# A hyena, conformer and attention encoder: its 64x64 transform done in pairs on quarters of TensorE

## The chip, the cores and the metric

The kernel runs on one core of a Trainium2 chip. The time is the device time of one execution in microseconds (us); every output is float32. One execution of each kernel is also profiled, and the rows below come from that.

## The reference, cut to what matters

One encoder layer runs over two request groups (x_prompt, x_sample) of 2048 positions and 1024 channels, with the same weights:

```
h = rmsnorm(x);  p = h @ w_in                         # 1024 -> 3584
hyena:     u, z = conv3(p_u) split in x0, x1, v
           k2 = two-sided filter from an MLP, on a circle of 4096, (4096, 512)
           y = x0 * (irfft(rfft(v*x1, 4096) * rfft(k2)) + skip*(v*x1))   # 512 channels
conformer: GLU, conv over 31 positions, layernorm, silu                 # 256 channels
attention: 4 heads of 64 into 256 memory tokens                         # 256 channels
out = rmsnorm(x + concat(y*silu(z) of the three) @ w_out)
```

The long convolution is the part that the change touches: a Fourier transform of 4096 points for each of 512 channels and two groups, a product with the filter's spectrum, and the inverse.

## The kernel before, in words

The 4096 points are a 64 x 64 matrix of n1 and n2. The two groups are taken as real and imaginary part of one complex sequence, so one transform serves both. It has four steps: stage A transforms over n1 for each n2 (result X1, in DRAM, by n2 and k1); stage B takes one k1 at a time, transforms over n2, multiplies with the filter's spectrum and transforms back over k2 (result AA, in DRAM, by k1 and n2); stage C transforms back over k1 for each n2 and goes on to the output.

The program has four stretches.

Stage 1 (0 to about 1370 us) is the projection h @ w_in in 5184 matmuls of 128x512 (lines 502 to 504), split in high and low parts. Beside it, queues of background steps (`fq` and others) give TensorE and the rest their small work: the conformer's convolution on VectorE (L276), the filter's MLP and its transform over n1 (`spec`, L400, into XF in DRAM, 16 calls), and the first 8 stage A's (`trans` in `a_background`). u = v*x1 goes to UU in DRAM at L558, for 4 tiles of channels and two groups.

Attention (about 1370 to 1516) has 16 blocks (`attention`, L841), of 512 positions each. Beside them come the other 24 stage A's (`stage_a`, L897), two for each of the first 12 blocks. A stage A transposes, multiplies in three split products (`times_t1`), moves its two PSUM results to SBUF, one on ScalarE and one on VectorE (L912), and stores them.

Stage B (about 1494 to 1682) has 33 steps t. Steps 1 to 31 handle k1 = t and k1 = 64-t, which share one spectrum, steps 0 and 32 one k1. `spectrum` makes K from XF with a full 128x128 matmul (L932) and copies it in four halves (L934 to L937). `unit` is then called for each k1: a full 128x128 matmul (L918), two copies that swap the halves of its result (L920, L921), u*kr on VectorE (L923), us*ki on VectorE or POOL (L924), their sum or difference on POOL (L925), the inverse matmul (L927), a copy (L928) and one store of 128 partitions x 2 KB. All these are float32 matmuls, which the trace shows as two instructions each. Every third step from t = 9 also loads and splits a slice of w_out (`wo_load`, L943; the splits are L234 on ScalarE and L235 on POOL). The last two blocks of attention are mixed with the first four steps of stage B.

Stage C (1682 to about 2104) has 32 steps n of two n2 each: it loads its slices of AA (`at`), of GG (the gate, `g8`), of x, transforms (L1034), transposes (L1039), gates (L1043), splits, and projects with w_out in 48 matmuls (L1057 to L1059), adds x and normalizes.

What sets the order: a scheduler at build time puts each engine's instructions in one list by estimated times; within `in_order()` the order in which the code is written holds for PE and ScalarE. Each engine executes its list in that order. Loads are issued on SP's queue, stores of stage B on ScalarE's. Eight semaphores serve the transfers of both queues in turn, and a transfer waits for the one that had its semaphore before to land. Tiles come from rings: a tile of a tag with bufs=n waits for the n-th one before it to be released.

## Time and profile before

| | us |
|---|---|
| median of three runs | 2107.04 |
| lowest and highest | 2104.28, 2109.05 |
| profiled execution | 2107.82 |
| its span in the trace | 2106.0 |
| PE busy | 1983.5 (94%) |
| DVE busy | 1233.5 (59%) |
| ACT busy | 780.4 (37%) |
| POOL busy | 847.8 (40%) |

PE is TensorE's matmuls, DVE VectorE, ACT ScalarE, POOL GpSimd, SP the engine that issues the loads. The times of PE count pipelined matmuls and are not a measure of its peak. The share of the span is an average over stretches with different limits, so the rows below are asked of single stretches.

### The profile page before, as it was taken

The page shows a single profiled execution, that of the slowest core. Times are in us where ns is not written, and L with a number is a line of the kernel's source. Part 1 is how long each engine was busy: PE and PEld are TensorE (multiplying, and loading weights), DVE is VectorE, ACT ScalarE, POOL GpSimd, SP SyncE. Part 2 cuts the span into 40 slices and gives each one's busy share as a digit, 9 for nine tenths or more (in the row PEclk, how much of TensorE's full clock was granted, in tenths as well). Part 3 has the DMA queues.
Part 4 walks back from the last instruction along what each step waited for, and adds up shares of the span by engine and source line. Part 5 has one row for each costly group of instructions (what it writes and reads, how often), then busy time and mean ns, then how long its engine had stood idle before and what let it go on. Part 6 is the DMA issues. An engine that isn't in the chain of part 4 may idle for free. (4 is left out here: it accounts for less than half of the span.)

```text
span 2106.0 us, 25970 instructions
## 1 busy us (share of the span) xinstructions
PE 1983.5 (94%) x8866; PEld 1500.1 (71%) x8866; DVE 1233.5 (59%) x1779; ACT 780.4 (37%) x1468; POOL 847.8 (40%) x838
## 2 busy tenths in 40 slices
PE   5999989998998999999998999899988899999998
PEld 5887778777887787777776877777533267777776
DVE  4533974959646379445448865278887624344443
ACT  4422112131335244444431222278688622222221
POOL 3332766554543222344434441266598711111110
PEclk8999999999999999999999999999999999999999
DMA  9634134342458323233341325698888685555552
GB/s 333 210 106 158 68 93 116 99 133 80 171 191 278 131 86 108 82 96 84 102 116 56 118 88 189 221 291 263 245 273 273 215 218 135 152 159 148 152 145 61
DMA packets 238558, 328.72 MB, mean 156 GB/s; under 512 B 87177, under 2 KB 117913, under 8 KB 236634
## 3 DMA queue, kind: packets, MB, share of 16 engines
q1 hardware_dynamic: 146026, 260.72, 38.9%
q10 hardware_dynamic: 87056, 54.57, 9.6%
q0 software_dynamic: 5344, 11.77, 2.0%
q8 instruction: 71, 1.16, 0.2%
q14 instruction: 61, 0.50, 0.1%
HBM read 196.37 MB, written 130.61 MB: 155 GB/s over the span
## 5 line engine op out<-in xcount | busy, mean ns | idle before, releaser
L502 PE MATMUL pj<-xh,whi 128*128 128x512 f32 (+1 forms) x1728 | 679.0, 393 | 23.6 <-ACT xh L468 6.7
L503 PE MATMUL pj<-xl,whi 128*128 128x512 f32 (+1 forms) x1728 | 673.4, 390 | 9.7 <-POOL xl L469 9.7
L504 PE MATMUL pj<-xh,wlo 128*128 128x512 f32 (+1 forms) x1728 | 671.8, 389 | 2.0 <-POOL wlo L235 2.0
L276 DVE SCALAR_TENSOR_TENSOR bg<-bg,vb,bg 128x512 f32<-128x512 f32 x480 | 399.0, 877 | 39.6 <-POOL bg L271 35.7
L502 PEld LDWEIGHTS pj<-xh,whi 128*128 128x128 f32 x1728 | 332.3, 193 | 105.2 <-ACT sm L516 15.0
L503 PEld LDWEIGHTS pj<-xl,whi 128*128 128x128 f32 x1728 | 332.8, 193 | 79.7 <-POOL xl L469 11.0
L504 PEld LDWEIGHTS pj<-xh,wlo 128*128 128x128 f32 x1728 | 332.5, 192 | 71.0 <-issue 3.6
L1057 PE MATMUL ms<-wo,mh 128*128 128x512 f32 x512 | 204.3, 399 | 2.2 <-ACT mh L234 2.2
L1058 PE MATMUL ms<-wo,mh 128*128 128x512 f32 x512 | 201.2, 393 | 0.0
L1059 PE MATMUL ms<-wo,ml 128*128 128x512 f32 x512 | 194.3, 397 | 0.2 <-POOL ml L235 0.2
L516 ACT COPY sm<-pj 128x512 f32<-128x512 f32 x96 | 56.5, 589 | 353.4 <-PE pj L504 272.0
L525 DVE SCALAR_TENSOR_TENSOR sm<-sm,va,sm 128x448 f32<-128x448 f32 (+1 forms) x96 | 77.7, 809 | 145.5 <-POOL sm L523 106.0
L544 POOL TENSOR_TENSOR big<-big,sm 128x448 f32<-128x448 f32 (+1 forms) x64 | 121.2, 1894 | 100.9 <-DVE sm L527 100.9
L1060 DVE TENSOR_TENSOR xr<-xr,ms 128x512 f32<-128x512 f32 x64 | 44.0, 688 | 199.0 <-PE ms L1059 198.9
L523 POOL TENSOR_SCALAR sm<-sm,va 128x448 f32<-128x448 f32 (+1 forms) x96 | 110.9, 1155 | 114.3 <-ACT sm L516 110.6
L241 POOL TENSOR_TENSOR ss<-ss,mhalf 128x1 f32<-128x1 f32 x32 | 17.7, 553 | 313.3 <-DVE ss L240 313.3
L1057 PEld LDWEIGHTS ms<-wo,mh 128*128 128x128 f32 x512 | 96.9, 189 | 47.4 <-issue 24.3
L1059 PEld LDWEIGHTS ms<-wo,ml 128*128 128x128 f32 x512 | 96.5, 188 | 21.0 <-DVE mf L1043 0.8
L1058 PEld LDWEIGHTS ms<-wo,mh 128*128 128x128 f32 x512 | 96.9, 189 | 20.0
L239 ACT ACTIVATE junk<-xr 128x1024 bf16<-128x1024 f32 x32 | 33.9, 1060 | 192.4 <-DVE xr L1060 185.9
L925 POOL TENSOR_TENSOR z<-z,us 128x512 f32<-128x512 f32 x64 | 81.9, 1289 | 31.3 <-DVE us L924 22.7
L235 POOL TENSOR_TENSOR wlo<-sm,whi 128x512 fp32r<-128x512 f32 x50 | 75.6, 1526 | 37.2 <-ACT whi L234 28.9
(169 smaller groups left out, 2758.6 us busy)
## 6 DMA issues: line engine op xcount, KB each, us to landing
big<-in_xt_dram SPq DMA_DIRECT2D x32, 512.0 KB, 6.8
in<-x1d SPq DMA_DIRECT2D x128, 128.0 KB, 3.6
aa<-o ACTq DMA_DIRECT2D x64, 256.0 KB, 3.5
at<-aa SPq DMA_DIRECT2D x64, 256.0 KB, 5.0
out_dram<-xr ACTq DMA_DIRECT2D x64, 256.0 KB, 3.8
sm<-in_win_dram SPq DMA_DIRECT2D x52, 256.0 KB, 3.6
ws<-whi SPq DMA_DIRECT2D x52, 256.0 KB, 3.0
ws<-wlo SPq DMA_DIRECT2D x52, 256.0 KB, 4.2
```

The source lines that it names most:

```text
L235: (sub_eng or nc.gpsimd).tensor_tensor(lo, src, hi.bitcast(F32), op=ALU.subtract)
L276: nc.vector.scalar_tensor_tensor(st["a", c], st["h", c][:, k:k + TB], vb[:, 2 * k + c:2 * k + c + 1], st["a", c], op0=ALU.mult, op1=ALU.add)
L502: nc.tensor.matmul(ps[:, ts_], hi, xh[:, k, ts_], start=k == 0, stop=False)
L503: nc.tensor.matmul(ps[:, ts_], hi, xl[:, k, ts_], start=False, stop=False)
L504: nc.tensor.matmul(ps[:, ts_], lo, xh[:, k, ts_], start=False, stop=k == KC - 1)
L523: nc.gpsimd.tensor_scalar(ct[:, o:e], pt[:, o + 1:e + 1], w[1], va[:, 52 + ch:53 + ch], op0=ALU.mult, op1=ALU.add)
L525: nc.vector.scalar_tensor_tensor(ct[:, o:e], pt[:, o:e], w[0], ct[:, o:e], op0=ALU.mult, op1=ALU.add)
L544: nc.gpsimd.tensor_tensor(v, v, out, op=ALU.mult)
L925: nc.gpsimd.tensor_tensor(z, z, us, op=op)
L1057: nc.tensor.matmul(po, mh[:, k, :], woh[k][:, hs], start=i == 0, stop=False)
L1058: nc.tensor.matmul(po, mh[:, k, :], wol[k][:, hs], start=False, stop=False)
L1059: nc.tensor.matmul(po, ml[:, k, :], woh[k][:, hs], start=False, stop=i == 7)
```

## The change

The n2 are taken in the order (0, 32), (1, 33), ... Stage A's two results of a pair are replaced by their sum and difference (`butterfly`): ScalarE copies one result, VectorE adds the other to it and then subtracts. `spec` does the same. So the transform over n2 is left with 32 pairs, once for the even and once for the odd k2, and what was one 128x128 matrix falls apart into 64x64 quarters.

Stage B has 32 steps, each with a pair of k1, t and `mirror(t)` (64-t, and 32 for 0). `forward` transforms both with four quarter matmuls into two banks; `multiply` makes four products on VectorE, straight from PSUM; `inverse` forms the complex sums in the accumulation of eight quarter matmuls, in one tile of two banks, which ScalarE copies in one instruction and POOL adds and subtracts; `store` writes each k1 with 64 partitions x 4 KB. `spectra` makes K for two steps at once. AA has 1024 columns and 64 rows for each k1. PSUM pools change (tr 3 to 4, one two-bank `pa`, no `po`: attention's result o sits in `tr`), rings too (`in` 8 to 9, `z` and `k` 8, `o` 4 of 1024). Stage B starts after the block loop. UU is written in two transfers for one; in stage C g8 has four loads of 256-byte runs for two of 512-byte runs, and indices follow the new n2 order.

```diff
+    def butterfly(a, b, px):
+        nc.scalar.copy(b, px[1])
+        nc.vector.tensor_tensor(a, px[0], b, op=ALU.add)
+        nc.vector.tensor_tensor(b, px[0], b, op=ALU.subtract)
...
     def spec(b, n):
+                butterfly(f[0], f[1], px)
                 for q in range(2):
-                    nc.scalar.copy(f[q], px[q])
                     nc.sync.dma_start(XF[n2p // 2, q * P:(q + 1) * P, :], f[q])
...
-        ms, tr, pa, po_ = psum(c2, ms=2, tr=3, pa=2, po=1)
+        ms, tr = psum(c2, ms=2, tr=4)
+        pap = c2.enter_context(tc.tile_pool(reuse_waits="tile", name="psa", bufs=1, space=PS))
...
     def stage_a(n):
-            px = pa(), pa()
+            px = pa().rearrange("p (s c) -> p s c", s=2)
+            px = px[:, 0, :], px[:, 1, :]
             times_t1(px, th, tl, uh, ul)
+            xo = t_z(), t_z()
+            butterfly(*xo, px)
             for s in range(2):
-                xo = tl_("us", 4)
-                (nc.scalar.copy if s else nc.vector.tensor_copy)(xo, px[s])
-                nc.scalar.dma_start(X1[2 * n + s, 0:128, :], xo)
+                nc.scalar.dma_start(X1[2 * n + s, 0:128, :], xo[s])
...
+        def quarters(banks, jobs):
+            n = len(jobs[0][3])
+            for j in range(n):
+                for b, c, r, ops in jobs:
+                    w, x = ops[j]
+                    nc.tensor.matmul(banks[b][c, :], w[r, :], x[r, :], start=j == 0, stop=j == n - 1)
+        def spectra(ts):
...
+            for j in range(2):
...
+                    pk = [tr() for _ in ts]
+                    quarters(pk, [(i, c, (lo_, hi_)[(i + h) % 2], [(stab[:, 2 + 2 * i + j, :], xfs[i])])
+                                  for i in range(len(ts)) for h, c in enumerate((lo_, hi_))])
+                for b, p in enumerate(pk):
+                    k = t_k()
+                    nc.scalar.copy(k, p)
...
+        def forward(st, t):
+            xa, xb = fetch(t), fetch(mirror(t))
+            st["u"] = u = ms(), ms()
+            w0, w1 = stab[:, 0, :], stab[:, 1, :]
+            quarters(u, [(0, lo_, lo_, [(w0, xa)]), (0, hi_, hi_, [(w0, xa)]),
+                         (1, lo_, hi_, [(w1, xb)]), (1, hi_, lo_, [(w1, xb)])])
+        def multiply(st):
+            for j in range(2):
+                for b in range(2):
+                    st["z", j, b] = t_z()
+                    nc.vector.tensor_tensor(st["z", j, b], st["u"][b], st["k", j, b], op=ALU.mult)
+        def inverse(st, t):
+            o = pa()
+            quarters((o[:, 0:TB], o[:, TB:]),
+                     [(h, c, r, [(stab[:, 6 + 2 * v + j, :], st["z", j, v]) for j in range(2)])
+                      for h, c, r, v in ((0, lo_, lo_, 0), (0, hi_, hi_, 1), (1, lo_, hi_, 0), (1, hi_, lo_, 1))])
+            eo, st["y"] = tl_("o", 4, 1024), tl_("o", 4, 1024)
+            nc.scalar.copy(eo, o)
+            for h, op in enumerate((ALU.add, ALU.subtract)):
+                nc.gpsimd.tensor_tensor(st["y"][:, h * TB:(h + 1) * TB], eo[:, 0:TB], eo[:, TB:], op=op)
+        def store(st, t):
+            for k, r in ((t, lo_), (mirror(t), hi_)):
+                nc.scalar.dma_start(AA[k, 0:64, :], st["y"][r, :])
+        def stage_b():
+            sts = [{} for _ in range(33)]
+            spectra([(sts[0], 0)])
+            forward(sts[0], 0)
+            for t in range(33):
+                with in_order():
+                    if t < 32:
+                        if t:
+                            forward(sts[t], t)
+                        multiply(sts[t])
+                    if t % 2 == 0 and t < 31:
+                        spectra([(sts[k], k) for k in (t + 1, t + 2) if k < 32])
+                    if t:
+                        inverse(sts[t - 1], t - 1)
+                    if t > 1:
+                        store(sts[t - 2], t - 2)
+                    if t >= 9 and t % 3 == 0 and t < 32:
+                        wo_load(t // 3 - 3)
+            store(sts[31], 31)
...
             attention(*blocks[n], qy)
             more_a(1)
-            if n >= 14:
-                more_b(2)
             qy = nq
-        more_b(33)
+        stage_b()
...
-                g8 = sp.tile([P, 4, 2, P], F32, tag="g8", name=nm("g8"))
+                g8 = sp.tile([P, 4, 2, 2, 64], F32, tag="g8", name=nm("g8"))
                 for g in range(2):
-                    nc.sync.dma_start(g8[:, :, g, :], chans(GG, g, n))
+                    for q in range(2):
+                        nc.sync.dma_start(g8[:, :, g, q, :], chans(GG, g, q, n))
```

On PE, the end of stage B of the kernel before has each step's three kinds of matmul (tr is the forward, ms the spectrum, pa the inverse), here in steps 30 to 32:

```order
L918 MATMUL tr_13395<-in_13392,stab 128x512
L927 MATMUL pa_13359<-z_13355,stab 128x512
L932 MATMUL ms_13419<-in_13416,stab 128x512
L927 MATMUL pa_13387<-z_13383,stab 128x512
L918 MATMUL tr_13431<-in_13428,stab 128x512
L918 MATMUL tr_13448<-in_13445,stab 128x512
L932 MATMUL ms_13464<-in_13461,stab 128x512
```

The changed kernel has on PE, in two steps near the start of stage B (ms is the forward, tr the spectra, pa the inverse; x2 is two quarters):

```order
L964 MATMUL ms_12110<-in_12104,stab 64x512 x2
L964 MATMUL ms_12111<-in_12107,stab 64x512 x2
L964 MATMUL tr_12130<-in_12124,stab 64x512 x2
L964 MATMUL tr_12131<-in_12127,stab 64x512 x2
L964 MATMUL tr_12140<-in_12124,stab 64x512 x2
L964 MATMUL tr_12141<-in_12127,stab 64x512 x2
L964 MATMUL pa_12150<-z_12082,stab 64x512
L964 MATMUL pa_12150<-z_12084,stab 64x512
```

Every step now issues its forward first, then the spectra for the next two steps (in every second step), then the inverse of the step before, whose second half uses two more z; in the kernel before the three kinds came in an order that varied.

On DVE, one block of attention with its two stage A's in the kernel before (L859 is attention's maximum, L865 and L872 its normalization, L879 its gate; L235 and L912 are stage A's):

```order
L235 TENSOR_TENSOR k_1488_10787<-tr_10781,k_1487_10786 128x512
L865 RECIPROCAL se_10854<-se_10854 128x2
L865 RECIPROCAL se_10872<-se_10872 128x2
L912 COPY us_10767<-pa_10759 128x512
L872 COPY ynp<-tr_10838 128x4x128
L859 TENSOR_REDUCE mx_10956<-ms_10951 128x2
L859 TENSOR_REDUCE mx_10974<-ms_10969 128x2
L912 COPY us_10798<-pa_10790 128x512
```

The same place on DVE in the changed kernel, where L257 and L258 are the butterfly's sum and difference, L894 the maximum, L900 and L907 the normalization, L914 the gate:

```order
L907 COPY ynp<-tr_10578 128x4x128
L257 TENSOR_TENSOR z_10394<-pa_10387,z_10395 128x512
L894 TENSOR_REDUCE mx_10739<-ms_10734 128x2
L258 TENSOR_TENSOR z_10395<-pa_10387,z_10395 128x512
L900 RECIPROCAL se_10718<-se_10718 128x2
L914 TENSOR_TENSOR ynp<-tr_10404,z_10402 128x512
L907 COPY ynp<-tr_10618 128x4x128
L894 TENSOR_REDUCE mx_10757<-ms_10752 128x2
L900 RECIPROCAL se_10740<-se_10740 128x2
L257 TENSOR_TENSOR z_10506<-pa_10499,z_10507 128x512
L894 TENSOR_REDUCE mx_10842<-ms_10837 128x2
L900 RECIPROCAL se_10758<-se_10758 128x2
```

One L912 copy of each stage A has become two instructions, with attention's maximum between them, and both of them read the same two-bank tile pa.

On ACT, in stage B of the kernel before (L920 and L921 swap halves, L928 moves the inverse, L936 a half of K):

```order
L936 ACTIVATE k_2107_12895<-ms_12892 64x512
L920 COPY us_12906<-tr_12904 64x512
L921 COPY us_12906<-tr_12904 64x512
L928 COPY o_12855<-pa_12868 128x512
L920 COPY us_12923<-tr_12921 64x512
L921 COPY us_12923<-tr_12921 64x512
L980 DMA aa<-o_12855 128x512
```

On ACT, in two steps of the changed stage B (k are the spectra of two steps, o<-pa is eo):

```order
L1025 COPY o_12195<-pa_12186 128x1024
L1031 DMA aa<-o_12160 64x1024 x2
L989 COPY k_12234<-tr_12228 128x512
L989 COPY k_12236<-tr_12229 128x512
L989 COPY k_12244<-tr_12238 128x512
L989 COPY k_12246<-tr_12239 128x512
L1025 COPY o_12257<-pa_12248 128x1024
L1031 DMA aa<-o_12196 64x1024 x2
```

The two stores of a step stand behind the copy of the next step's inverse, and the seven half and full copies of a step before have become three on the mean.

## Rows read from the trace of the kernel before

**Rows 1.** Busy by stretch: length, PE, PEld, DVE, ACT, POOL, clock, DMA, GB/s
```profile
1378.00:1478.00 100.00, 100.00 (x756) 71.85 (x753) 82.42 (x166) 80.02 (x263) 61.52 (x77) 1.00 0.84 269
...
1516.00:1682.00 166.00, 140.74 (x296) 52.43 (x294) 126.49 (x176) 126.92 (x223) 138.46 (x107) 0.98 0.80 256
1682.00:1698.00 16.00, 9.77 (x35) 6.44 (x36) 1.09 (x3) 2.42 (x4) 1.30 (x1) 0.81 0.84 216
1698.00:2088.00 390.00, 389.51 (x1722) 293.71 (x1723) 155.45 (x215) 86.82 (x153) 56.92 (x61) 0.99 0.56 147
```

**Rows 2.** Groups by line in stage B: busy us, mean ns, idle before
```profile
L925 POOL TENSOR_TENSOR z<-z,us 128x512 f32<-128x512 f32 x61 | 78.1, 1290 | 25.1 <-DVE us L924 16.5 <-PE tr L918 2.6 <-PE pa L927 1.9
...
L923 DVE TENSOR_TENSOR z<-tr,k 128x512 f32<-128x512 f32 x60 | 41.0, 689 | 20.1 <-ACT us L921 12.7 <-POOL z L925 2.8 <-PE pa L927 2.6
L928 ACT COPY o<-pa 128x512 f32<-128x512 f32 x60 | 34.9, 587 | 12.5 <-PE pa L927 10.6 <-ACT o L928 0.8
...
L235 POOL TENSOR_TENSOR wo<-in,wo 128x512 fp32r<-128x512 f32 x16 | 21.5, 1352 | 2.4 <-ACT wo L234 2.3
```

**Rows 3.** Waits of stage B, 1516 to 1682: us in total, times, longest
```profile
PEld pa L927 <- POOL z L925: 21.9, 24, 3.2
...
POOL z L925 <- DVE us L924: 16.5, 10, 6.4
```

**Rows 4.** Waits of SP's queue, 1515 to 1682
```profile
SPq L954 <- DMA aa<-o: 30.5, 23, 4.9
```

**Rows 5.** DMA of stage B: total, issues, KB each, us to landing
```profile
DMA packets 24101, 42.43 MB, mean 256 GB/s; under 512 B 3831, under 2 KB 3831, under 8 KB 23957
...
aa<-o ACTq DMA_DIRECT2D x60, 256.0 KB, 3.5
in<-x1d SPq DMA_DIRECT2D x106, 128.0 KB, 3.5
```

**Rows 6.** Timeline of DVE: starts of L879, the end of an attention block
```profile
1468.91 0.69 DVE L879 TENSOR_TENSOR ynp<-po,o 128x512 f32<-128x512 f32 x1
...
1477.86 0.69 DVE L879 TENSOR_TENSOR ynp<-po,o 128x512 f32<-128x512 f32 x1
...
1485.22 0.69 DVE L879 TENSOR_TENSOR ynp<-po,o 128x512 f32<-128x512 f32 x1
...
1492.32 0.69 DVE L879 TENSOR_TENSOR ynp<-po,o 128x512 f32<-128x512 f32 x1 [0.33 <-PE po L877]
```

**Rows 7.** Timeline of PE in stage 1, about a spec
```profile
778.08 1.09 PE L405 MATMUL ms<-f,f 64*64 64x512 f32 x8
779.10 0.70 PE L356 MATMUL ms<-f,wf 128*128 128x256 f32 x2
```

**Rows 8.** Line 937 from 1540 to 1682: ns min/median/max, first and last start
```profile
L937 DVE COPY k<-ms x24: 694/695/696, 1542.5 to 1676.0; 64x512 f32<-64x512 f32 x24
```

**Rows 9.** Busy time by stretch, first 52 us
```profile
0.00:52.00 52.00, 27.82 (x153) 26.26 (x154) 22.86 (x53) 25.08 (x54) 15.94 (x20) 0.87 0.94 332
```

**Rows 10.** Page, group of L239
```profile
L239 ACT ACTIVATE junk<-xr 128x1024 bf16<-128x1024 f32 x32 | 33.9, 1060 | 192.4 <-DVE xr L1060 185.9
```

**Rows 11.** Page, DMA issues: KB each, us to landing
```profile
out_dram<-xr ACTq DMA_DIRECT2D x64, 256.0 KB, 3.8
```

**Rows 12.** Line 980: ns of one issue, min/median/max
```profile
L980 ACTq DMA_DIRECT2D aa<-o x33: 326/327/361, 1503.2 to 1682.7; - x33
```

**Rows 13.** Chain of waits at the end of stage B
```profile
1680.07 1.98 PE pa L927 x2
1682.07 0.59 ACT o L928
1682.69 5.59 DMA aa<-o
```

**Rows 14.** Busy time by stretch, second half of stage 1
```profile
700.00:1370.00 670.00, 651.62 (x2885) 513.85 (x2884) 383.30 (x529) 235.97 (x327) 233.93 (x283) 0.99 0.36 112
```

More of the change, by code (lines that the diff above doesn't have):

```diff
@@ new lines, in inverse, with both @@
+    def inverse(k2, conj, turned):
+        th = 2 * np.pi * ((k2[:, None] * ab.T) % 64) / 64
+        w = np.zeros((2, 32, 2, 32))
+        re = np.stack([np.cos(th), np.sin(th)], axis=1)
+        im = conj * np.stack([-np.sin(th), np.cos(th)], axis=1)
+        w[0], w[1] = (im, -re) if turned else (re, im)
+        return w.reshape(64, 64)
+    def both(a, b):
+        return np.concatenate([a, b], axis=0)
+    ev, od, evr, odr = 2 * jj, 2 * jj + 1, 62 - 2 * jj, 63 - 2 * jj
+    fk = both(forward(ev), forward(od))
@@ new lines, in _tables @@
+    kr, ki = np.tile(fk[:, :32], 2), np.tile(fk[:, 32:], 2)
+    turn = np.roll(np.arange(128), 64)
+    stab = np.stack([both(forward(ev), forward(od)), both(forward(evr, -1.0), forward(odr, -1.0)),
+                     kr, ki, kr[turn], ki[turn]] + [
+        both(inverse(ev, 1.0, u), inverse(od, 1.0, u)) for u in (False, True)] + [
+        both(inverse(odr, -1.0, u), inverse(evr, -1.0, u)) for u in (False, True)], axis=1)
+    sk = np.zeros((2, 32, 2, 4, 2, 2, 32))
+    for h in range(2):
+        k2 = 2 * jj + h
+        th, al = 2 * np.pi * ab * k2 / 64, np.pi * ab / 64 + 2 * np.pi * ab * k2 / 64
+        sg = (-1.0) ** h
+        g0, g1 = (np.cos(al), -np.sin(al)), (-sg * np.sin(al), -sg * np.cos(al))
+        for c_ in range(2):
+            for v in range(2):
+                sk[h, :, 0, 2 * c_, h, v] = (np.cos(th), -np.sin(th))[c_]
+                sk[0, :, 1, 2 * c_ + 1, h, v] = (g0[c_] + g1[c_]) / 2
+                sk[1, :, 1, 2 * c_ + 1, h, v] = (g0[c_] - g1[c_]) / 2
@@ new lines @@
+        lo_, hi_ = slice(0, 64), slice(64, 128)
+        def quarters(banks, jobs):
[5 more added lines that the diff above has]
+        def spectra(ts):
+            xfs = []
+            for i, (_, t) in enumerate(ts):
+                xfs.append(t_in())
+                src = XF[:, 0:256, :].rearrange("m (h e k) c -> m h e k c", h=2, e=4)
+                for h in range(2):
+                    r = 64 * ((h + i) % 2)
+                    nc.sync.dma_start(xfs[i][r:r + 64, :], src[:, h, :, t, :])
+            if ts[0][1] == 0:
+                sk = t_in().rearrange("p (j c) -> p j c", j=4)
+                nc.sync.dma_start(sk, a["sk"])
+            for j in range(2):
+                if ts[0][1] == 0:
+                    pk = tr(), tr()
+                    for b in range(2):
+                        nc.tensor.matmul(pk[b], sk[:, 2 * j + b, :], xfs[0], start=True, stop=True)
+                else:
+                    pk = [tr() for _ in ts]
[4 more added lines that the diff above has]
+                    nc.scalar.copy(k, p)
+                    if ts[0][1] == 0:
+                        ts[0][0]["k", j, b] = k
+                    else:
+                        ts[b][0]["k", j, 0] = ts[b][0]["k", j, 1] = k
```

136 lines of the change are left out of this document (45 added, 91 removed).

## The prediction

> **What bounds the kernel now.** I read the busy time by stretch first [rows 1]. Attention (1378 to 1478 us) keeps TensorE busy 100.00 of 100 us at full clock; stage C (1698 to 2088) 389.51 of 390. Between them lies stage B, 1516 to 1682, in which no engine is full: PE 140.74 of 166, DVE 126.49, ACT 126.92, POOL 138.46. The chain of waits runs through the end of stage B, the landing of its last store and into stage C [rows 13], so whatever shortens stage B shortens the kernel one for one, and whatever attention loses is lost one for one.
>
> What holds stage B is read next from its groups and waits. Its costliest group is POOL's add, 61 x 1290 ns [rows 2], and PE's largest wait is for just that: 21.9 us before the inverse matmul, while POOL itself waited 16.5 us for DVE's product [rows 3]. The loading queue on SP waited 30.5 us, in 23 places, for an earlier store to land [rows 4]. So three things share it: a long chain through four engines, POOL, and the DMA traffic at 256 GB/s [rows 5]. The rate of the stage is read from the one DVE copy that comes once a step: 24 of them from 1542.5 to 1676.0, so 133.5 / 23 = 5.80 us a step [rows 8].
>
> **The change part by part.** The new step T handles the same two k1 in 32 steps; I price each engine.
>
> PE: forward is four f32 64x64 quarters, inverse eight, the spectra eight in every second step (the order of PE shows the rows). Stage 1 has such quarters already: eight instructions, which are four f32 matmuls of two passes, take from 778.08 to 779.10, 1.02 us [rows 7]. So a group of four costs 1.02; a step has 1 + 2 + 1 (mean) groups, 4.1 us; a step with spectra 5.1, one without 3.1.
>
> DVE: four products of PSUM and K at 689 ns (L923 [rows 2]), 2.8 us. The copies to K and the DVE half of us*ki go. But both `ms` banks are held until the last two products have read them, and the next forward rewrites them: forward 1.1 + 4 x 0.69 = 3.9 us is a floor of each step. So pairs of steps take 5.1 + 3.9, mean 4.5.
>
> ACT: two copies of spectra at 587 ns (as L928 [rows 2]) and one of 128x1024, for which the nearest row is the 1060 ns of L239 [rows 10]: 2.2 us, and under 3 with the casts of w_out. POOL: two ops at 1290 ns and 16 splits of w_out at 1352 [rows 2] over 32 steps: 2.6 + 0.7 = 3.3 us.
>
> DMA: per step four X1 loads of 128 KB, two of XF, two stores of 256 KB and half a w_out load of 256 KB: 1408 KB, 1.44 MB. At the 256 GB/s of now that takes 5.6 us; at the 332 GB/s that the first 52 us reach, at a share of 0.94 [rows 9], 4.35. The share of now is 0.80 [rows 1]; stage B's own traffic at 0.94 would be 256 x 0.94 / 0.80 = 301 GB/s, 4.8 us. A store is now 64 partitions of 4 KB where it was 128 of 2 KB; out_dram<-xr has the new form and lands in 3.8 us against 3.5 [rows 5, 11]. The buffer named o turns over in two steps: issue of both stores 0.7 (two of the 0.33 that one takes now [rows 12]), landing 3.8, POOL 2.6, which is 7.1 in 2T, so 3.6 a step, no bound as long as a landing is short.
>
> So the bounds are 4.5 (PE with DVE), 3.3 (POOL), 4.35 to 5.6 (DMA). I take T = 4.8: above PE's bound, at what the DMA does at a 0.94 share, as the nearest row for the rate is stage B's own traffic.
>
> Start: of the present order, blocks 14 and 15 are mixed with stage B; now they are not. DVE's last instruction of block 11 (L879) stands at 1477.86, a block's length of 8.95 after 1468.91 [rows 6]; blocks without stage A take 7.1 (1485.22 to 1492.32 [rows 6]), so four at some 7.2, with what stage B's first loads and products take beside them, end at 1506.7. Stage B then ends at 1506.7 + 32 x 4.8 = 1660.3, against the 1682.05 at which the last inverse is done now [rows 13]: -21.8.
>
> What is added: (1) Attention. Each of the 24 stage A's there has one more DVE op, two in each of 12 blocks. DVE's 82.42 of 100 us [rows 1] is 7.4 of a block's 8.95; two more at 0.69 make 8.8, so DVE has no slack left beside a full PE, and the matmul's two banks are held through ACT copy, add and subtract (2.0 us) instead of one copy of 0.7. Nothing if it all fits, 12 x 1.0 if DVE becomes the bound with its waits (17.6 idle of 100 now) half kept; I take +5. What is queued behind such a wait on DVE is attention's maximum, which PE's transposes wait for. (2) The end: eo 1.06 and two POOL ops of 1.29 and a second store's issue of 0.33 behind the last inverse, where now one copy of 0.59 stands [rows 13]: +3.4, not hidden, since the first load of stage C needs every k1. (3) Stage 1: 16 spectra with two DVE ops more, 22 us, and one ACT op less; DVE has 383 busy of 670 there [rows 14], so 0, with 3 either way for the order. (4) Stage C: GG in 256-byte runs and twice the loads, under a PE that is full at a DMA share of 0.56 [rows 1]: 0, with 2 either way. (5) Two writes of UU for one, 8 times, on ACT's queue: below 0.5 each beside full PE, 0.
>
> Sum against the profiled run's own 2107.82 (span 2106.0): -21.8 + 5 + 3.4 = -13.4, so 2094.4. That run lies 0.8 above the median of the three, so I say 2094.
>
> **The rivals.**
>
> *PSUM and DVE alone bound it* (T = 3.9). If the transfers follow on demand, and the spectra's extra groups fit beside the DVE chain, the step falls to the floor of 3.9. For it: the loading queue is three steps ahead with nine `in` tiles, and 332 GB/s was reached once. Against: PE's mean of 4.1 is above it and 1.44 MB / 3.9 is 370 GB/s. 1506.7 + 124.8 + 8.4 = 1639.9, so -42: 2066. The Trainium skill, "TensorEngine Tiling (Array Packing)", section "PSUM Bottleneck", says that tiling speeds TensorE but not the emptying of PSUM, which may then be the bottleneck: by that rule the four products of DVE set the step, and this rival's time is what it gives; the L923 row agrees as to DVE's price and cannot show more.
>
> *DVE holds attention* (+12 instead of +5): -21.8 + 12 + 3.4 = -6.4, so 2101. For it: 8.8 of 8.95. Against: the idle time of DVE there is spread over short waits that two ops can fill.
>
> *The stores hold stage B*, on the other side. Its place is o's ring and SP's waits for a store. In o's ring the POOL add of step t+2 waits for the store of step t to land; with a landing of 7.2 us, twice the 3.5 of now, (0.7 + 7.2 + 2.6) / 2 = 5.25, and the eight semaphores that the program gives its transfers in turn, of which stores take a quarter, hold the loads as [rows 4] shows. It decides from T = 5.2 on: 1506.7 + 5 + 3.4 + 32 x 5.2 = 1681.5, as now. At 256 GB/s, 5.64 a step, it ends at 1695.6: +13.5, 2121. For it: stage B has stood at 256 GB/s with the same bytes, and 64-partition stores are two for one. Against: these 256 GB/s were at 5.8 us a step with engines waiting for one another; out_dram<-xr lands in 3.8. The Trainium skill, "SBUF — State Buffer", section "Can I just issue two DMAs to hit both halves?", says that two transfers of 64 partitions each do not reach together what one of 128 does, since each sees half the ports: by that the stores run at about half speed, and this rival's 2121 follows. The trace agrees only in part: stage B's 106 X1 loads of 64 partitions, 14 MB of its 42 [rows 5], did not keep it from 256 GB/s, and the 3.8 us of out_dram<-xr is 9% above the 3.5, not double.
>
> *The change doesn't do what it says*: quarters that do not run side by side in stage B, or a clock at the lower of its two levels (a mean of 0.81 was granted in the 16 us of the gap [rows 1]). A group at 2.04 makes 8.2 a step, some +100. Stage 1's row and 0.98 in stage B speak against it.
>
> **How the numbers follow.** Forecast (T 4.3 to 5.1, 2079 to 2104): 52%. The fast rival 15%, DVE in attention 10%, the stores 18%, quarters or clock 5%. A difference under 0.2%, 4.2 us, is none that a measurement of this kernel can tell. Faster: 52 + 15 and most of attention's 10, less the edge of the forecast, 74%. Same: 8%, from the step near 5.1 to 5.3. Slower: 13 of the stores' 18 and 5 of the last, 18%. Range: from the fast rival's neighbourhood, 2069, to near the stores' 2121, 2118; the likeliest case's own range is 2079 to 2104.
>
> **What would show it.** In the profile after: the distance between the 128x1024 copies on ACT is T (4.8 forecast; in turns of 5.1 and 3.9 if PE and DVE set it, even if the DMA does). DVE products near 0.69 and groups of four quarters at 1.02. If DMA is the bound, PE waits for `in` and SP for `aa<-o`; if the stores are, POOL waits for DMA aa<-o and the landing is over 6 us. DVE in attention: blocks of over 9.4 us prove the second rival. A stage C other than 390 us, or a stage 1 that moved by over 3, would prove terms (3) and (4) wrong.

## The result, and the profile after

The changed kernel takes 2136.93 us in the median of four runs (2132.51 to 2138.36), the kernel before 2108.05 beside it: a ratio of 1.0143, 95% interval 1.0128 to 1.0157. It is 1.4% slower, where 2094 was forecast with a range up to 2118. The profiled execution has a span of 2136.6 us against 2106.0.

The 30.6 us are read off at four marks. The first two are the last projection matmul of the kernel before (L504) and of the changed kernel (L531), with durations in ns and first and last start:

```profile
L504 PE MATMUL pj<-xh,wlo x1728: 278/389/1415, 19.6 to 1357.4; 128*128 128x512 f32 x177, 128*128 128x256 f32 x15
```

```profile
L531 PE MATMUL pj<-xh,wlo x1728: 278/389/1415, 17.8 to 1371.9; 128*128 128x512 f32 x177, 128*128 128x256 f32 x15
```

Stage 1 ends 14.5 us later. The next mark is the gate that ends an attention block, L879 before and L914 after:

```profile
L879 DVE TENSOR_TENSOR ynp<-po,o x16: 677/692/692, 1378.9 to 1516.5; 128x512 f32<-128x512 f32 x16
```

```profile
L914 DVE TENSOR_TENSOR ynp<-tr,z x16: 672/683/693, 1398.3 to 1530.3; 128x512 f32<-128x512 f32 x16
```

The first block ends 21.5 us after the projection before and 26.4 after. Twelfth and first gate of the changed kernel, in the timeline of DVE, show the blocks with stage A (before: 1378.88 to 1477.86, 9.00 each [rows 6]):

```profile
1398.26 0.69 DVE L914 TENSOR_TENSOR ynp<-tr,z 128x512 f32<-128x512 f32 x1 [1.93 <-DMA z<-zx]
...
1507.34 0.68 DVE L914 TENSOR_TENSOR ynp<-tr,z 128x512 f32<-128x512 f32 x1
```

That is 109.08 / 11 = 9.92 us a block, 10.1 us more in all. The last four blocks, no longer mixed with stage B, take 22.9 for 38.6. The step of stage B is the distance of the 128x1024 copies on ACT:

```profile
L1025 ACT COPY o<-pa x32: 1004/1012/1056, 1536.4 to 1707.0; 128x1024 f32<-128x1024 f32 x32
```

170.6 / 31 = 5.50 us a step, where 4.8 was forecast and 5.80 stood before [rows 8]. Stage C's first transform comes 16.5 us after the last of these copies starts, at 1723.46, and from there to the end are 413.1 us (412.6 before). So the sum is +14.5 (stage 1), +4.9 (ahead of the first block), +10.1 (blocks), -15.7 (last four), +16.2 (from the last gate, 1530.3, to stage C: 193.2 against 177.0 before), +0.5 (stage C) = 30.5, the 30.6 but for rounding. Two of these marks move by themselves: in the runs whose stage 1 is the changed kernel's own, the last projection starts between 1370.2 and 1376.2, and in those whose attention is its own, a block takes 9.71 to 9.92.

Busy time by stretch after, with the columns of [rows 1] (the DMA column is the mean busy share of the DMA engines). The first stretch is taken inside the blocks, since at 1378 the changed kernel has not ended its first block:

```profile
1410.00:1500.00 90.00, 84.13 (x621) 60.25 (x620) 75.89 (x157) 67.36 (x219) 53.24 (x66) 0.98 0.75 237
...
1520.00:1716.00 196.00, 154.26 (x1077) 55.66 (x1075) 85.84 (x138) 78.69 (x126) 104.56 (x85) 0.95 0.84 257
...
1732.00:2110.00 378.00, 378.00 (x1677) 285.39 (x1675) 122.56 (x210) 98.95 (x149) 81.80 (x60) 1.00 0.59 148
```

In stage B DVE, ACT and POOL do less than before (85.84, 78.69 and 104.56 of 196 us, against 126.49, 126.92 and 138.46 of 166), PE is busy for 154.26, and the DMA moves about the same, 257 GB/s. In attention PE fell from all of the time to 84.13 of 90 us, 93%, and DVE is at 84% where it was at 82%. Stage B's largest waits, SP's issues of X1 loads (ns, min/median/max), and the shares of the chain that ended last from 1520 to 1740:

```profile
POOL o L1027 <- DMA aa<-o: 62.5, 22, 5.1
DVE z L1017 <- ACT k L989: 42.8, 17, 6.4
DVE z L1017 <- PE ms L964: 41.4, 23, 4.5
```

```profile
L1000 SPq DMA_DIRECT2D in<-x1d x124: 507/597/2042, 1521.6 to 1693.8; - x124
```

```profile
by line: DMA in<-x1d 17.0%; PE pa L964 14.9%; PE ms L964 7.5%; PE tr L964 7.2%; DMA in<-xf 6.9%; ACT k L989 6.3%; issue 5.2%; ACT o L1025 5.2%; DMA aa<-o 3.7%; ACTq L1031 3.0%; DMA at<-aa 2.8%; SPq L974 2.8%; SPq L1000 2.2%; PE ms L1138 1.7
```

The loads (x1d and xf) stand in that chain with 24%, the landings of the stores with 4%.

Summed over the trace from 1550 to 1700, SP's 169 issues take 126.6 us, 0.75 each, and 50 of them take over 0.8; in the kernel before 173 issues from 1520 to 1676 take 95.1, 0.55 each, and 2 are over 0.8. At 6.7 issues a step that is 5.0 us of issuing in a step of 5.50. The long issues follow the stores: 45 of the 50 begin within 2.5 us of the start of a store's issue on ACT (86 issues do, 0.90 us in the mean), and 5 are among the other 83 (0.60 in the mean); in the kernel before none of the 130 that stand so behind a store is over 0.8. The prediction priced the loads by their bytes alone.

### The profile page after: what moved, and what is told of

Read it like the earlier page. It is cut to its first block, busy times and chain, and to the rows that moved or that the text cites. A ratio compares the mean times of both kernels' runs of the same rounds, so it can differ in the third digit from the quotient of the medians.

```text
span 2136.6 us, 27090 instructions
## 1 busy us (share of the span) xinstructions
PE 1981.7 (93%) x9568; PEld 1495.8 (70%) x9568; DVE 1179.5 (55%) x1775; ACT 724.2 (34%) x1325; POOL 837.5 (39%) x807
## 3 DMA queue, kind: packets, MB, share of 16 engines
q1 hardware_dynamic: 162906, 260.59, 38.6%
## 4 chain that ended last, share of the span: by engine, by line
PE 61%; DVE 12%; DMA 9%; issue 7%; POOL 5%; ACT 4%; SPq 1%; ACTq 1%; POOLq 0%; DVEq 0%
PE pj L529 11%; PE pj L530 11%; PE pj L531 11%; DVE bg L303 7%; PE ms L1138 6%; PE ms L1139 5%; PE ms L1140 5%; DMA in<-x1d 2%; PE pa L964 2%; PE tr L1115 2%; DMA bg<-in_x_sample_dram 1%; POOL big L571 1%; DMA z<-zx 1%; PE ms L674 1%; POOL wlo L262 1%
## 5 line engine op out<-in xcount | busy, mean ns | idle before, releaser
L531 PE MATMUL pj<-xh,wlo 128*128 128x512 f32 (+1 forms) x1728 | 671.4, 389 | 6.9 <-POOL wlo L262 6.8
L531 PEld LDWEIGHTS pj<-xh,wlo 128*128 128x128 f32 x1728 | 332.5, 192 | 76.6 <-POOL wlo L262 9.1
L1017 DVE TENSOR_TENSOR z<-ms,k 128x512 f32<-128x512 f32 x128 | 80.9, 685 | 94.5 <-ACT k L989 42.8
L1027 POOL TENSOR_TENSOR o<-o 128x512 f32<-128x512 f32 x64 | 79.9, 1271 | 86.8 <-DMA aa<-o 62.5
```

Of the source, the lines that this page charges most:

```text
L531: nc.tensor.matmul(ps[:, ts_], lo, xh[:, k, ts_], start=False, stop=k == KC - 1)
L1017: nc.vector.tensor_tensor(st["z", j, b], st["u"][b], st["k", j, b], op=ALU.mult)
L1027: nc.gpsimd.tensor_tensor(st["y"][:, h * TB:(h + 1) * TB], eo[:, 0:TB], eo[:, TB:], op=op)
```

## The experiments

The runs are told by what they ask. Times are medians; the kernel before lies at 2106 to 2108 beside all of them, and the figures in brackets are the ratio to it and its 95% interval. A step is the distance of the 128x1024 copies over all 32, a block the mean of eleven with stage A, each read as above. In the code, "..." marks lines of an edit that are left out.

### Stage B: number and form of transfers

**fetch1.** X1 is laid out by (h, n), so that one load of 128 partitions replaces two of 64.

```diff
-            for h, r in enumerate((lo_, hi_)):
-                nc.sync.dma_start(x[r, :], src[:, h, :, t, :])
...
+            nc.sync.dma_start(x, src[:, :, t, :])
```

> The changed kernel with one edit: X1 is laid out so that one load of 128 partitions x 2 KB brings what two loads of 64 partitions bring, so SP issues 2 transfers less in each step of stage B (4.7 for 6.7), with the same bytes. Theory S (SP's queue is the bound): the step falls from 5.5 to 4.6 to 4.9 us, the kernel to 2112 to 2120. Rival B (257 GB/s is the bound): the step stays at 5.3 to 5.6, the kernel at 2130 to 2140.

2114.4 us (1.0043, 1.0029 to 1.0057), and a step of 4.66: as theory S had it. One stretch of the changed kernel, then of fetch1:

```profile
1545.00:1672.00 127.00, 103.71 (x751) 36.35 (x747) 58.18 (x92) 52.77 (x82) 69.38 (x56) 0.97 0.85 260
```

```profile
1545.00:1672.00 127.00, 116.03 (x870) 47.16 (x865) 68.64 (x109) 62.27 (x96) 83.66 (x68) 0.97 0.94 303
```

With the same bytes the DMA goes from a share of 0.85 to 0.94 and from 260 to 303 GB/s: the 301 GB/s that the prediction worked out are reached, with fewer transfers. POOL's wait for the stores fell with it, from 62.5 to 31.5 us, though the stores were not touched; SP's mean issue stayed at 0.74 us.

**fetch1_tiny.** Behind each of fetch1's loads, one of 64 rows of 16 bytes into a tile that nothing reads.

```diff
             nc.sync.dma_start(x, src[:, :, t, :])
+            nc.sync.dma_start(tl_("tiny", 8, 4)[0:64, :], X1[:, 0, 0:4])
```

> The kernel fetch1 (X1 read in one load of 128 partitions where there were two of 64), with one load of 64 rows of 16 bytes added behind each of these loads, into a tile that nothing reads: the number of SP's issues and of transfers on the shared semaphores is again 6.7 a step, the bytes and the form of the large loads stay. Theory S (number of issues on SP's queue): the step goes back from 4.66 us to 5.2 to 5.6, the kernel to 2130 to 2140. Rival P (the 64-partition form of a load is what was slow): the step stays at 4.6 to 4.8, the kernel at 2112 to 2118.

2141.36 us (1.0154, 1.0133 to 1.0174), step 5.58. The scheduler let the tiny loads run ahead, so that all are issued by 1600.7; one execution then shows both cases, busy time before and after:

```profile
1550.00:1600.00 50.00, 32.71 (x212) 10.13 (x212) 15.59 (x25) 15.51 (x25) 19.32 (x16) 0.83 0.69 188
1600.00:1690.00 90.00, 82.12 (x576) 33.03 (x576) 44.86 (x71) 42.96 (x68) 55.83 (x46) 0.98 0.93 300
```

While they are issued, three for each X1 load, the DMA moves 188 GB/s, though the large loads have the form of fetch1; when they are gone, 300. So more issues on the same queue are enough to make the step long. That the 64-partition form of a load costs nothing of its own is not shown: no run has that form with fewer transfers, and rows of 16 bytes are not the changed kernel's. What of it is SP's time to issue and what is the wait of a transfer for its semaphore's last user is not told apart either.

**pair2k.** AA is laid out by pairs of k1, so that the two stores are 128 partitions x 2 KB each.

```diff
-            for k, r in ((t, lo_), (mirror(t), hi_)):
-                nc.scalar.dma_start(AA[k, 0:64, :], st["y"][r, :])
+            for h in range(2):
+                hs = slice(h * TB, (h + 1) * TB)
+                nc.scalar.dma_start(AA[t, 0:P, hs], st["y"][:, hs])
...
```

> The changed kernel with AA laid out by pairs of k1, so that the two stores of a step are 128 partitions x 2 KB each, with the 128 rows at one stride; the loads of stage B are untouched, stage C reads AA in the pairs' order. Theory F (the stores of 64 partitions x 4 KB make SP's issues long): SP's mean issue falls from 0.75 us to 0.55 to 0.6, the step from 5.5 to 4.8 to 5.0, the kernel to 2117 to 2124. Rival L (the long issues come with the load on the DMA engines, whatever the form): SP's mean issue stays at 0.7 or more and the step within 0.2 of 5.5, the kernel at 2132 to 2140.

2123.69 us (1.0078, 1.0057 to 1.0099), step 5.10, a little above what theory F gave. From 1560 to 1680 SP's mean issue is 0.60 us, 11 of 153 over 0.8, with the same number of transfers and untouched loads. With fetch1, where the issues stayed long at a DMA share of 0.94, this shows that the form of the stores makes the loads' issues long; the form was worth 0.4 us a step, half of what the loads' number was worth.

**store_128x2k.** The same two stores without a new layout: the destination is two blocks of 64 rows far apart.

```diff
-            for k, r in ((t, lo_), (mirror(t), hi_)):
-                nc.scalar.dma_start(AA[k, 0:64, :], st["y"][r, :])
+            m = mirror(t)
+            for h in range(2):
+                hs = slice(h * TB, (h + 1) * TB)
+                nc.scalar.dma_start(AA[t:m + 1:m - t, 0:64, hs], st["y"][:, hs])
```

> The changed kernel with one edit in stage B: the two stores of a step are not 64 partitions x 4 KB each, one for each k1, but 128 partitions x 2 KB each, one for each half of the columns, as the kernel before had them. Bytes and number of transfers are the same. Theory S (SP's queue is the bound: its issues take 0.75 us in the mean against 0.55 before, 50 of 169 over 0.8, because the stores in the new form hold up the making of the loads' descriptors): issues fall to 0.55 to 0.6, the step from 5.5 to 4.7 to 5.0 us, the kernel to 2115 to 2124. Rival B (the DMA engines move no more than 257 GB/s whatever the form): the step stays at 5.3 to 5.6, the kernel at 2130 to 2140. Rival O (the ring of o waits for a store to land): the landing of aa<-o falls below 4 us and POOL's wait for it from 62 us to under 20.

A miss of all three theories: 2366.75 us (1.124, 1.1221 to 1.1258).

```profile
1560.00:1900.00 340.00, 207.41 (x858) 57.94 (x849) 68.33 (x108) 60.95 (x95) 83.94 (x68) 0.73 0.34 112
```

12.08 us a step with the DMA engines at a share of 0.34, and POOL waits 269.8 us for the stores. The only difference of these stores to pair2k's is that the 128 rows of the destination are 2 x 64 and not at one stride. The DMA packets of the trace show what is slow. The queue that carries the stores, from 1600 to 1900:

```profile
q10 hardware_dynamic: 6180, 12.46, 10.7%
```

10.7% of 16 engines' time is 1.7 engines. From 1600 to 1860 us two packets of this queue run at once for 68% of the time and never more than four, where pair2k has up to 19 at once. So such a store is moved two packets at a time, and two stores of 256 KB at that rate (2 KB in 83 ns) make 10.7 us, most of the step. The runs do not show why a transfer is dealt out so.

**yn_late.** The four 1 MB loads of the conformer's result move from the end of the last attention block to steps 1, 3, 5 and 7.

> The changed kernel with one edit: the four loads of 1 MB of the conformer's result are not issued on SP's queue at the end of attention's last block but one by one behind steps 1, 3, 5 and 7 of stage B. Theory Y (these loads wait on SP for attention's last operations and hold the loads of stage B behind them): the gap of 12.0 us between the first and the second 128x1024 copy (1536.4 to 1548.5) falls to 5 to 7, the kernel by 4 to 8 to 2129 to 2133. Rival (the 4 MB cost their time on the DMA engines wherever they stand): what the start gains the next eight steps lose, the kernel at 2134 to 2140.

2138.04 us (1.0145, 1.0121 to 1.0169): the time is the rival's, and theory Y is out, for the gap that should have closed grew to 15.1 us (1538.6 to 1553.7). The rival's own reason, that what the start gains is lost later, is not shown either, since the start gained nothing.

### Stage 1: the second write of UU

**uu_spread.** Each half of UU is written at its own block of positions (tb 1 and tb 3). A half is written before all of it is computed, so it is a measure of time alone.

```diff
-                if tb == NB - 1:
-                    for q in range(2):
...
+                if tb % 2:
+                    q = tb // 2
...
```

> The changed kernel with one edit in stage 1: the two writes of UU of a tile are not issued one behind the other at its end, but each when its half of the positions is there (tb 1 and tb 3). Theory U (the second of two back-to-back UU writes keeps ACT's queue for 3.5 us, 8 times, and the copies that empty TensorE's results wait behind it): both issues fall to about 0.5 us, and the last projection matmul, which came 14.6 us later than in the kernel before (1371.9 against 1357.4), comes 9 to 14 us earlier; the kernel takes 2123 to 2128 instead of 2137. Rival (the two DVE operations of each spectrum have shifted the order of stage 1): the last projection stays within 3 us of 1371.9, the kernel at 2134 to 2140.

2124.55 us (1.0088, 1.0069 to 1.0108); the last projection at 1358.7. **bf_uu** puts the split alone into the kernel before:

```diff
-                    nc.scalar.dma_start(UU[i]...[:, :, g, :], st["u"]...)
+                    for q in range(2):
+                        nc.scalar.dma_start(UU[i]...[:, q * 32:q * 32 + 32, g, :], st["u"][:, q * 1024:(q + 1) * 1024]...)
```

> The kernel before with one part of the change alone: each of the 8 writes of UU is split in two halves of the positions, issued one behind the other on ACT's queue. Theory U: the second issue of each pair takes about 3.5 us, the last projection matmul comes 9 to 14 us later than 1357.4, the kernel takes 2115 to 2121. Rival (it was the spectra's butterfly or the order): the last projection stays within 4 us of 1357.4, the kernel within 4 of 2107.

2124.39 us (1.0085, 1.006 to 1.011), a little more than theory U gave; the last projection at 1375.8, 18.4 later. The changed kernel's first UU write shows why, in the timelines of ACT and of PE; the last line is PE at the same place in the kernel before:

```profile
269.00 4.19 ACTq L586 DMA_DIRECT2D uu<-big  x2
273.31 0.59 ACT L543 COPY sm<-pj 128x512 f32<-128x512 f32 x1 [19.04 <-DVE bg L303]
```

```profile
273.95 0.80 PE L529 MATMUL pj<-xh,whi 128*128 128x512 f32 x1 [9.56 <-ACT sm L543]
```

```profile
272.83 0.80 PE L502 MATMUL pj<-xh,whi 128*128 128x512 f32 x1 [5.97 <-ACT sm L516]
```

The first issue takes 0.62 us of these 4.19, the second 3.5. Behind it on ACT's queue stands the copy that empties the projection's PSUM bank. PE waited for that copy before, too, 5.97 us; now it waits 9.56, longer by the 3.5 us of the second issue. Before, one write took 0.52 to 0.60 us to issue. In uu_spread each of 16 issues takes 0.52 to 0.62 again.

### Attention

**y_in.** The gate tile y comes from the ring of input tiles (`y = t_in()`) and no more from z.

> The changed kernel with one edit in attention: the tile y, into which the gate is loaded from ZX, comes from the ring of nine input tiles, which is idle there, and no more from the z ring that stage A's results fill and hold until their stores land. Theory R (the shared ring makes the loads of y late): the waits for z<-zx go, a block with stage A takes 9.0 to 9.3 us instead of 9.9, the kernel 2127 to 2132. Rival D (VectorE is the bound with its 8.8 us of work in a block): a block stays at 9.7 to 10.0, the kernel at 2134 to 2139.

2143.7 us (1.0179, 1.0161 to 1.0196). A block fell to 9.50 (1396.19 to 1500.69), 0.2 to 0.4 below the kernels with this part unchanged, a little of theory R. But the last four blocks took 30.7 us for 22.9, and stage B, whose first loads use that ring, had its first 128x1024 copy 15 us later.

**a_copies.** The butterfly beside attention replaced by two copies; it leaves out the sums and differences and is a measure of time alone.

> The changed kernel, with stage A's butterfly in attention left out (its 24 results are moved by one ScalarE copy and one VectorE copy as in the kernel before, so what is stored is not the sum and the difference). The tile y still comes from the z ring. Theory D (VectorE's extra operation and its chain behind ScalarE's copy set the attention blocks): a block with stage A falls from 9.92 us to 9.0 to 9.2, the kernel to 2123 to 2130. Rival R (the shared ring makes y late, whatever VectorE does): a block stays at 9.6 to 9.9, the kernel at 2133 to 2138.

2140.31 us (1.0152, 1.0135 to 1.0169), a block 10.23: neither theory. DVE is busy 62.44 of the 90 us from 1410 on, less than the changed kernel's 75.89, and yet PE waits longer for attention's copy on it:

```profile
PE tr L912 <- DVE ynp L907: 9.6, 6, 3.1
```

In the changed kernel PE's waits in the same stretch are:

```profile
PE tr L912 <- DVE ynp L907: 2.7, 8, 0.4
PE tr L245 <- DVE ynp L914: 1.9, 1, 1.9
PE pa L252 <- DVE z L258: 1.2, 2, 0.6
```

So PE waits there for attention's instructions in DVE's list more than for the two banks (the last line). **attn_psum**, with the pools of before during attention:

> The changed kernel with the PSUM pools of the kernel before while attention runs (tr 3, two single banks pa, one po for attention's result), and its own pools only from stage B on; the butterfly and the z ring stay. Theory Q (attention's result in the tr pool and stage A's result in one two-bank tile hold TensorE back): a block with stage A falls from 9.9 us (9.7 to 9.9 in the kernels with this part unchanged) to 9.0 to 9.4, the kernel to 2128 to 2133, less what stage B loses by starting behind the change of pools (0 to 4). Rival (the pools are not it): a block stays at 9.6 to 9.9, the kernel at 2134 to 2141.

2153.84 us (1.022, 1.0196 to 1.0244), a block 11.94: neither. In both the scheduler wrote another order, so parts of the change were put into the kernel before, one at a time.

**bf_ring** (y shares the ring of stage A's results) and **bf_psum** (o in tr):

> The kernel before with one part of the change alone: attention's gate tile y comes from the ring that stage A's results fill (8 tiles, as z in the changed kernel; the ring of input tiles is cut from 8 to 5 to make room, which can slow stage B by some us). Theory R (the stores of stage A's results make y late): waits for the load from ZX show, a block goes from 9.0 to 9.3 to 9.6 us. Rival: a block stays under 9.2.

> The kernel before with one part of the change alone: attention's result o is in the pool tr (now 4 banks) and no more in a bank of its own. Theory Q (the shared pool holds TensorE back): a block goes from 9.0 to 9.3 to 10 us, the kernel to 2110 to 2119. Rival: a block stays under 9.2, the kernel within 3 of 2107.

Blocks of 9.05 and 9.04; kernels 2116.18 (1.005, 1.0032 to 1.0068; its smaller ring of input tiles is in stage B) and 2107.26 (1.0, 0.9988 to 1.0011). Neither of them makes a block long.

**bf_bfly**, the butterfly alone (its stage B goes on with the old transform, so it is a measure of time alone):

```diff
-                (nc.scalar.copy if s else nc.vector.tensor_copy)(xo, px[s])
...
+            nc.scalar.copy(xo[1], px[1])
+            nc.vector.tensor_tensor(xo[0], px[0], xo[1], op=ALU.add)
+            nc.vector.tensor_tensor(xo[1], px[0], xo[1], op=ALU.subtract)
```

> The kernel before with one part of the change alone: the 24 stage A's beside attention end in the butterfly (copy, sum, difference) instead of two copies; stage B still takes its full transform, so what it computes from these is not the reference's. Theory D (the extra VectorE operation and the longer hold of the two banks make attention's blocks long): a block goes from 9.0 to 9.5 to 10.0 us, the kernel from 2107 to 2113 to 2119. Rival (there is room for it beside a full TensorE): a block stays under 9.2, the kernel within 3 of 2107.

2145.2 us (1.0189, 1.0167 to 1.0211), a block 10.64, both above what was expected; the last four blocks, mixed with stage B, took 59.5 us for 38.6. The timeline of PE of the kernel before, and then of bf_bfly, shows a second thing beside the butterfly:

```profile
1424.61 0.50 PE L231 MATMUL pa<-k,th 64*128 64x512 f32 x2
1424.95 0.40 PE L231 MATMUL pa<-k,tl 64*128 64x512 f32 x2
1425.18 0.39 PE L231 MATMUL pa<-k,th 64*128 64x512 f32 x2
```

```profile
1426.19 0.50 PE L231 MATMUL pa<-k,th 64*128 64x512 f32 x1
1426.53 0.39 PE L231 MATMUL pa<-k,tl 64*128 64x512 f32 x1
1426.76 0.39 PE L231 MATMUL pa<-k,th 64*128 64x512 f32 x1
1428.58 0.49 PE L231 MATMUL pa<-k,th 64*128 64x512 f32 x1
```

Before, the matmuls of the two halves of TensorE's rows run side by side (x2); here one result is finished first and the halves run one after the other. Of the 144 such matmuls beside attention 140 start side by side before, 6 in bf_bfly. The same holds for attn_psum with its two single banks: 6 of 144. With the one two-bank tile of the change all 144 do.

**bf_bfly_2bank** keeps them too:

> The kernel before with the butterfly of stage A beside attention, as in bf_bfly, but with stage A's two results in one two-bank tile, as the changed kernel has them. In bf_bfly the scheduler pulled the matmuls of the two halves of TensorE's rows apart (3 and 3, none side by side), which alone costs some 2 x 3 x 0.33 = 2 us a block; with one tile they stay in pairs. Stage B uses one half of that tile and can only lose; what it computes is not the reference's. Theory D (the butterfly itself is slow: one more VectorE operation, banks held longer): a block takes 9.5 to 10.0 us, as the 9.9 of the changed kernel. Rival P (only the lost pairs made bf_bfly slow): a block takes 9.0 to 9.2.

A block takes (1488.72 - 1382.25) / 11 = 9.68 us with all in pairs: theory D, in the tile of the change. The kernel is at 2144.96 (1.0184, 1.0169 to 1.0199); its stage B, which has half of pa, is not compared.

### A version faster than both

**best3** joins fetch1, one load of XF in every second step, one store of 128 partitions x 4 KB a step (AA by pairs), the second UU write on SP's queue, and y from the ring of o.

> The changed kernel with five edits together: X1 read in one load of 128 partitions, XF of every second step too, the two stores of a step in one of 128 partitions x 4 KB (AA by pairs), the second UU write on SP's queue, y from the ring of o. By the parts: stage B at the DMA rate of fetch1 (303 GB/s, 4.66 us a step) saves 22 to 24 us, stage 1 gives back 9 to 13, attention 3 to 8; the kernel takes 2093 to 2103 and is faster than the kernel before (2106). If SP's queue cannot bear the second UU write, stage 1 gives nothing back, and it takes 2106 to 2112.

2100.2 us (0.9966, 0.9952 to 0.9981). **best4** adds yn_late, **best5** to that the pools of attn_psum:

> The kernel best3 with the four loads of the conformer's result moved into steps 1 to 7 of stage B. Best3 has 16.7 us between attention's last product and the first 128x1024 copy, and SP stands 28 us in the queue of those loads. Theory Y: that distance falls to 6 to 9, the kernel from 2100 to 2091 to 2096. Rival (the bytes only move): 2098 to 2102.

> The kernel best4 with the PSUM pools of the kernel before while attention runs. If theory Q holds, a block falls from 9.49 us to 9.0 to 9.2 and the kernel by 4 to 6 from best4; if not, it stays within 3 of best4, or loses up to 4 by the change of pools between attention and stage B.

2099.91 (0.9973, 0.9961 to 0.9985) and 2108.03 (1.0006, 0.9994 to 1.0017): best4 gains nothing on best3, and best5 loses 8 us, more than either of its cases. A block of best5 takes 10.43, with its pairs lost (6 of 144). **best6** is best4 with a butterfly that asks VectorE for one operation:

```diff
-            butterfly(*xo, px)
+            nc.scalar.copy(xc, px[1])
+            nc.scalar.activation(xm, px[1], AF.Copy, scale=-2.0)
+            nc.vector.tensor_tensor(xo[0], px[0], xc, op=ALU.add)
+            nc.gpsimd.tensor_tensor(xo[1], xo[0], xm, op=ALU.add)
```

> The kernel best4 with another butterfly beside attention: ScalarE copies one result and writes it again times -2, VectorE adds it to the other, and POOL forms the difference from the sum and the -2 copy, in SBUF; so VectorE has one operation a stage A, as in the kernel before, and the two banks are free after one VectorE operation. Theory D: a block falls from 9.48 us to 9.0 to 9.2, the kernel by 3 to 6 from best4 to 2094 to 2097. If ScalarE's or POOL's added operation comes to be waited for instead, a block stays at 9.4 or above and the kernel within 3 of best4.

2077.88 us (0.9866, 0.9849 to 0.9882), 1.3% faster than the kernel before. Its busy time in stage B and in attention:

```profile
1517.00:1648.00 131.00, 120.44 (x976) 49.58 (x968) 76.53 (x123) 70.39 (x105) 94.00 (x76) 1.00 0.93 321
1390.00:1470.00 80.00, 79.94 (x603) 57.78 (x602) 65.17 (x134) 72.36 (x233) 72.02 (x81) 1.00 0.89 277
```

PE is full in attention again, a block takes 9.00, though ACT and POOL rose to 90%. Stage B runs at 321 GB/s and 4.23 us a step. The kernel is 22 us below best4 where 3 to 6 were expected. The 0.48 us a block make 5.3 of it; the distance between the last gate and the first 128x1024 copy fell from 15.6 us to 6.2 and the last four blocks by 2.3. That part was not expected, and the runs do not say what it hangs on.

## Why the prediction was wrong

**The step that failed first is "I take T = 4.8", the term of DMA.** It was worked out from bytes and a rate. The rate, 301 GB/s at a share of 0.94, was right (fetch1: 303 at 0.94), but the change's own transfers, as many as before in less time and the stores in a form that lengthens SP's issues, do not reach it: 5.50. That is 32 x 0.70 = 22 us. The trace of the kernel before had rows for it: SP's issues took 0.55 us each, 6.7 a step, 3.7 of the hoped-for 4.8. Nothing in the sum stood for them; at 0.55 they would still have fitted, at the 0.75 that they came to they make 5.0.

**The UU term (5), "0", measured +14.5** (18.4 alone). It put each of the two issues below 0.5 us, and the second took 3.5; eight of these are 28 us, of which stage 1 felt about half. The cover it named, a full PE, was not there: at the first write PE had stood idle 5.97 us for the copy behind the issue already. Terms (3) and (4) held: uu_spread, with the spectra's butterfly still in, ends stage 1 1.3 us after the kernel before, and stage C moved by 0.5.

**Attention, "+5", measured +10.1 in the blocks and +4.9 ahead of the first.** That the butterfly makes a block long is shown (bf_bfly_2bank: 9.68 with it; best6: 9.00 in the same tile with one DVE operation less), and a share of the shared ring of y is seen in y_in. Which part of its mechanism does it is not told apart: best6 takes away the second DVE operation and the longer hold of the two banks together, and the waits of PE for the banks are 1.2 us of the 90, those for attention's instructions on DVE 4.6. DVE was not full: it is busy 84% of the blocks, 8.4 us of each, a little less than the 8.8 that the prediction added up. The rival "DVE holds attention" had the size, 12, and its sign, blocks of over 9.4, came true, though it was put at 10%.

**Right were** the direction of the rival "the stores hold stage B" and its place: T is 5.50, beyond its point of 5.2, and POOL waited 62.5 us for the store's landing. Its price was not. A landing takes 4.5 us in the median, not 7.2, and its sum for o's ring left out a term: over steps 4 to 27 a store is issued 2.8 us in the mean after POOL has its result, since on ACT it stands behind the next step's copy. With that, 0.5 for the first of the two issues, the measured landing and POOL's 2.5, an estimate is (2.8 + 0.5 + 4.5 + 2.5) / 2 = 5.2 us a step, so o's ring was nearly as long as the step; with fewer loads (fetch1) the 2.8 falls to 0.7. No run gives o more tiles, so what the ring alone costs stays open; the larger cause that an edit showed is the number of loads.

The prices of the compute engines held: products at 0.685, the 128x1024 copy at 1.012 for 1.06. A group of four quarters takes 0.86 in a run of them, not 1.02, as the chain of waits of the changed kernel has it:

```profile
1551.50 0.91 PE ms L964 x8
1552.41 1.72 PE tr L964 x16
```

So the 4.5 us that PE and DVE were to need was too high as well: best6 stands at 4.23. The rule of the Trainium skill ("SBUF — State Buffer", "Can I just issue two DMAs to hit both halves?") that two 64-partition transfers do not reach what one of 128 does agrees with fetch1 and pair2k in sign. Beside it the runs show two other costs: the number of issues (fetch1_tiny), and for the stores the longer issues of the loads behind them (pair2k). How much of either gain is the form itself no run here shows.

The start was 1511.7 in the prediction (1506.7 and 5) and 1530.3 in the trace: 14.5 of stage 1, 4.9 and 5.1 of attention, less 5.9, since the last four blocks took 5.7 each and not 7.2. The end took 16.5 us from the last inverse to stage C's first transform against 11.4, +5.1 for +3.4.

Open are a_copies, whose blocks were slower without the operation than with it, and the start of stage B in best4 and best6. With each edit the scheduler writes another order, and no run holds the order fixed.

## What to carry to other kernels

Price a stream of transfers by bytes and by the issues on the queue that starts them, and the turn of its ring with the wait for the issue in it; a speed-up of the engines leaves these where they were (here 4.8, 5.0 and 5.2 us against a step of 5.50). A store or load that is split in two costs an issue on a queue that other work stands behind: read what comes next on that queue before calling it free. Where a scheduler orders the instructions, read whether pairs that ran side by side still do (x2 or x1 in the timeline) before blaming the operation that was added.

## What was not expected of the hardware

The second of two back-to-back writes of UU, each with 128 partitions x 32 runs of 128 bytes, took 3.3 to 3.8 us to issue where the first took 0.4 to 0.6 (the changed kernel and bf_uu); issued on two queues (best6) both took under 1 us. SP's load issues went from 0.55 to 0.75 us in the mean beside stores of 64 partitions x 4 KB, and to 0.60 with 128 x 2 KB; the long ones came just behind a store's issue on the other queue. A store whose 128 rows are two blocks of 64 far apart was moved two packets at a time and gave 12.08 us a step against 5.10 for rows at one stride, with the DMA engines at 0.34.
